# Start-up of a decayed cumulative sum of x @ w: another deal of channels to partitions, w by row sets, and other cuts of x

## The chip, the core and the metric

The kernel runs on one core of a Trainium2 chip. The metric is the device time of one execution in microseconds (us). Three executions of the kernel before took 902.97, 903.10 and 903.15 us, the median is 903.1. One more execution was profiled; all durations below come from it. A core has the matrix engine (PE, with its weight loads shown apart as PEld), the vector engine (DVE), the scalar engine (ACT), GpSimd (POOL) and a sync engine (SP) that here only issues transfers. ACT, POOL and SP each have a queue of DMAs.

## What is computed

```python
def reference(x, w, decay):          # x (16, 2048, 1024), w (1024, 1024), decay (1024), float32
    B, S, D = x.shape
    xw = x @ w
    out = np.zeros_like(xw)
    out[:, 0, :] = xw[:, 0, :].copy()
    for t in range(1, S):
        out[:, t, :] = decay[None, :] * out[:, t - 1, :] + xw[:, t, :]
    return out.astype(np.float32)
```

So there is one matrix product and then, for each output channel, a first-order recurrence over time.

## The kernel before

**Tiles.** Time is cut into chunks of 512 steps, 64 in all; two neighbouring chunks make a group. The product is made in bf16 with output channels on the partitions: a tile is 128 output channels by the 1024 steps of a group, eight tiles a group. One tile takes 16 matmuls of 512 columns: eight slices k of 128 input channels for each of the two chunks. For this x must stand with input channels on the partitions and time along the row.

**x.** `load` (L105) brings a chunk in four DMAs on POOL's queue, one for each quarter q of the input channels (256 of them) into 32 partitions; time runs over the 32 partitions and over j, 16 blocks of 32 steps. The DMA turns float32 into bf16. `turn` (L115) is DVE's transpose of 32 by 32 blocks, over pairs of bf16 taken as one 4-byte element; m counts four groups of 32 such pairs. Its result is `xw`, in which the even and the odd channel of a pair stand next to each other. `part` (L123) copies `xw` apart into `xt` (first all even, then all odd channels). A matmul (L131) reads either `xw` with a step of two (`pairs`) or `xt`. In the steady state one transpose handles a whole chunk (128 x 2048 elements), and there are 62 of those.

**w.** For a matmul the row of `wsb` on partition p must be the input channel that x has there. Before the change, partition 32q + i of slice (m, e) holds channel 256q + 64m + 2i + e. w comes in four pieces, by half h of the output channels and by e (even or odd input channels). `load_w` (L319) issues four DMAs a piece, one for each quarter q of 32 partitions, with the four m in it: 128 rows of 512 float32, 262 KB read. Piece (0, 0) goes as float32 over the queues of SP and ACT, two DMAs each; the other three pieces go over POOL's queue and arrive as bf16. `settle` (L326) copies a slice from its staging place to `wsb`; the even slices of the first half can only be settled when all four DMAs of their piece have landed.

**The recurrence.** A tile's sum is scanned on DVE, either directly from PSUM (L229) or in a paired form, in which ACT copies the tile from PSUM (L191, `p`), multiplies the even steps (L171, `g` and `h`), POOL adds (L205 and L266) and DVE scans half as many steps (L210). Then DVE transposes back (L278) and SP's queue stores.

**Order.** Every instruction is pinned to the order in which it is written. The first 49 steps and the last 20 follow an `agenda` written out by hand; entry -99 is the start. Its letters: M loads a part of x, U a piece of w on POOL's queue, w and W settle a slice on ACT or DVE (Q and q half a slice each), E transposes one m of a part, F and G copy one m to `xt` on DVE or ACT, K a small copy and matmul that wait for a quarter of x, L loads a quarter of a later chunk, R and D bring the decays. `cuts` says how the first two chunks are cut: chunk 0 into 10 and 6 blocks, chunk 1 into 7 and 9. Entry 3 holds the next work: among others `p0 g0` on ACT and then `w9 w10 w11`, three even slices of the second half of w, and `W8`, `W12` to `W15` on DVE.

**PE's start.** `spin` (L344) runs five matmuls with zeros in float32; the first one waits for ACT's copy into `seed` (L337), which stands behind ACT's two DMA issues and a table load. One more spin waits for `gate`, a copy that ACT makes when the last quarter of x's first part is there. Then step 0 runs the first half's four tiles on chunk 0 (`firsts`, in the parts of `cuts[0]`, all even slices of a part before the odd ones) and chunk 1 (`seconds`). In the second part of chunk 1 the first two tiles read `xw` and the other two `xt`. Step 4, the first with the second half of w, takes its even slices first.

**POOL's queue.** The built program gives the DMAs of this queue eight semaphores in turn: the ninth issue waits for the landing of the first, the tenth for that of the second, and so on.

Of the kernel before, what the change touches and what calls it, by code (L numbers as in the profile page):

```python
# [25 lines left out]
def kernel(  # L26
# [41 lines left out]
    CR = CH // NQ  # L68

# [40 lines left out]
    def turn(c, j0=0, j1=NJ, m0=0, m1=M):  # L110
        if c not in xw_of:
# [4 lines left out]
            out=dst.rearrange("p (m j i) -> p j m i", m=M, i=P)[:, j0:j1, m0:m1],  # L116
            in_=src.rearrange("p (j m c) -> p j m c", m=M, c=P)[:, :, m0:m1]))
# [168 lines left out]
    class Outlet:  # L286
# [8 lines left out]
        def store(self, b, t0):  # L295
# [4 lines left out]
            for j in range(0, self.nj, nj):  # L300
# [11 lines left out]
    stage = {(0, 0): room[0][:, 0:size],  # L312
             (0, 1): room[0][:, size:size * 3 // 2].bitcast(BF16),
             (1, 0): room[1][:, 0:size // 2].bitcast(BF16),
             (1, 1): room[1][:, size // 2:size].bitcast(BF16)}

    def load_w(queues, h, e):
        for i, q in enumerate((0, 2, 1, 3)):
            pin(queues[i % len(queues)].dma_start(  # L319
                out=stage[h, e][quad(q)].rearrange("p (m d) -> p m d", m=M),  # L320
                in_=_ap(w, [[2 * D, P], [2 * P * D, M], [1, CH]],
                        (q * CQ + e) * D + h * CH)))

    def settle(h, e, m, copy, r0=0, r1=R):
        src = stage[h, e][:, m * CH:(m + 1) * CH]
        pin(copy(out=wcols[:, 2 * m + e, h][:, :, r0:r1],  # L326
                 in_=src.rearrange("p (q r i) -> p q r i", q=NQ, r=R)[:, :, r0:r1]))
# [6 lines left out]
    load_w((nc.sync, nc.scalar), 0, 0)  # L334
# [11 lines left out]
    spin(5, seed, wide)  # L346
    H = NJ // 2
    cuts = (((0, H + 2), (H + 2, NJ)), ((0, H - 1), (H - 1, NJ)))
    cols = const.tile([128, 2, P], FP32, name="cols")

    def load_half(i):
        for q in range(NQ):
            load(i // 2, q, *cuts[i // 2][i % 2])
# [5 lines left out]
    def load_part(i):  # L359
        load_w((nc.gpsimd,), *((0, 1), (1, 0), (1, 1))[i])  # L360

    def part_one(i, copy):
        part(i // 8, copy, i % 4, i % 4 + 1, *cuts[i // 8][i // 4 % 2])
# [126 lines left out]
    def turn_and_load(c):  # L490
# [22 lines left out]
        "E": lambda i: turn(i // 8, *cuts[i // 8][i // 4 % 2], i % 4, i % 4 + 1),  # L513
# [132 lines left out]
    for step, (g, n) in enumerate(slots):  # L646
# [11 lines left out]
        if step == 0:  # L658
# [109 lines left out]
```

## Time and profile before

| what | us |
|---|---|
| median of three executions | 903.1 |
| the profiled execution's own time | 902.81 |
| its span, first to last recorded event | 901.0 |
| PE busy | 894.4 |
| DVE busy | 825.5 |
| ACT busy | 685.4 |
| POOL busy | 657.6 |

A group's row of the profile gives the line, the engine, the operation, its operands as out<-in with partitions x elements and type, how many there were, their busy time and the mean of one in ns, and the idle time before them with what ended it. A row of the timeline gives start, length, engine, line, operation and count of a run of instructions, and in brackets the idle time just before it. The sums that follow are made against the profiled execution; what is outside its span (1.81 us) is taken to stay.

Each DMA of the start, in float32 bytes read: a quarter of x takes 32.8 KB a block (10 blocks 328 KB, 6 blocks 197 KB), each w DMA 262 KB.

### The profile page before, as it was taken

To read this page: it belongs to the slowest core of one execution; us is meant where nothing else is said; L and a number is where in the kernel's file an instruction comes from. 1 tells how busy PE (TensorE), PEld (TensorE's weight loads), DVE (VectorE), ACT (ScalarE), POOL (GpSimd) and SP (SyncE) were. 2 spreads that over 40 slices of the span, in tenths; PEclk is the share of its full clock that TensorE was granted. 3 is DMA by queue.
4 is the path that set the end of the run, shared out by engine and by line. 5 is a ranking of instruction groups with operands and counts; after the bars stand their busy time and mean duration, and the time that the engine had idled before them with its cause. 6 is when DMAs were issued, how large, how long until landed. Compare 5 with 4: busy or idle time off the path is not lost.

```text
span 901.0 us, 12290 instructions
## 1 busy us (share of the span) xinstructions
PE 894.4 (99%) x4211; PEld 412.9 (46%) x4211; DVE 825.5 (92%) x635; ACT 685.4 (76%) x957; POOL 657.6 (73%) x758
## 2 busy tenths in 40 slices
PE   8999999999999999999999999999999999999998
PEld 5444444444444444444444444444444444444444
DVE  4899989999999999999998999989999999999998
ACT  4888878777877877877778778777787787787843
POOL 8887878877767768677677687777777777776532
PEclk9999999999999999999999999999999999999999
DMA  9999999999999999999999999999999999999648
GB/s 193 188 205 246 242 210 215 215 236 236 255 253 253 258 241 257 254 243 233 219 242 220 227 235 219 238 222 227 239 226 224 226 237 227 228 222 220 186 133 242
DMA packets 402798, 204.77 MB, mean 227 GB/s; under 512 B 9008, under 2 KB 401712, under 8 KB 402736
## 3 DMA queue, kind: packets, MB, share of 16 engines
q0 software_dynamic: 137024, 68.70, 57.5%
q1 hardware_dynamic: 265424, 134.76, 56.9%
q8 instruction: 33, 0.54, 0.2%
q10 hardware_dynamic: 288, 0.52, 0.2%
q14 instruction: 29, 0.24, 0.1%
HBM read 138.42 MB, written 134.22 MB: 303 GB/s over the span
## 4 chain that ended last, share of the span: by engine, by line
PE 99%; ACT 0%; ACTq 0%; DVE 0%; issue 0%
PE ps L131 97%; PE spare L131 1%; PE spare L344 1%; ACT L337 0%; PE ps L413 0%; PE spare L413 0%; ACTq L319 0%; DVE h L442 0%; ACT seed L337 0%
## 5 line engine op out<-in xcount | busy, mean ns | idle before, releaser
L131 PE MATMUL ps<-xt,wsb 128*128 128x512 bf16 (+2 forms) x4048 | 867.8, 377 | 0.0
L131 PEld LDWEIGHTS <-wsb 128*128 128x128 bf16 x4184 | 408.2, 98 | 477.0 <-issue 0.3
L205 POOL TENSOR_TENSOR xs<-h,xs 128x512 f32<-128x512 f32 (+1 forms) x190 | 242.6, 1278 | 181.8 <-ACT h L171 82.5
L278 DVE STREAM_TRANSPOSE ot<-so 128x1024 f32<-128x1024 f32 (+2 forms) x264 | 300.5, 1175 | 3.1 <-POOL so L266 2.2
L191 ACT COPY xs<-ps 128x1024 f32<-128x1024 f32 (+1 forms) x190 | 188.7, 994 | 149.6 <-PE ps L131 142.3
L266 POOL TENSOR_TENSOR so<-h,xs 128x512 f32<-128x512 f32 (+1 forms) x189 | 240.9, 1275 | 40.4 <-ACT h L171 27.4
L123 ACT COPY xt<-xw 128x2048 bf16<-128x2048 bf16 (+4 forms) x136 | 242.5, 1789 | 6.2 <-DVE xw L115 6.2
L105 POOL DMA_DIRECT2D xb<-in_x_dram x264 | 174.3, 661 | 8.4 <-DMA xb<-in_x_dram 3.5
L171 ACT ACTIVATE h<-so,dec 128x512 f32<-128x512 f32 (+1 forms) x189 | 144.8, 766 | 29.5 <-DVE so L210 26.2
L115 DVE STREAM_TRANSPOSE xw<-xb 128x2048 f32<-128x2048 f32 (+4 forms) x78 | 147.3, 1900 | 6.7 <-DMA xb<-in_x_dram 6.7
L210 DVE TENSOR_TENSOR_SCAN so<-spare,keep,xs 128x512 f32<-128x512 f32 (+1 forms) x97 | 119.8, 1239 | 26.5 <-POOL xs L205 25.9
L210 DVE TENSOR_TENSOR_SCAN so<-spare,xs 128x512 f32<-128x512 f32 x93 | 113.2, 1219 | 25.9 <-POOL xs L205 22.4
L171 ACT ACTIVATE h<-ps,dec 128x512 f32<-128x512 f32 (+1 forms) x190 | 129.5, 683 | 0.0
L229 DVE TENSOR_TENSOR_SCAN so<-dec,ps 128x1024 f32<-128x1024 f32 x34 | 76.9, 2261 | 0.8 <-ACT h L171 0.6
L229 DVE TENSOR_TENSOR_SCAN so<-dec,keep,ps 128x1024 f32<-128x1024 f32 (+2 forms) x35 | 74.9, 2140 | 0.8 <-PE ps L131 0.8
L270 ACT COPY keep<-so 128x1 f32<-128x1 f32 x136 | 25.3, 189 | 9.3 <-DVE so L229 8.7
L201 ACT COPY so<-keep 128x1 f32<-128x1 f32 x97 | 18.4, 191 | 4.3 <-DVE ot L278 4.1
L131 PE MATMUL spare<-xt,wsb 128*128 128x512 bf16 (+5 forms) x60 | 12.8, 330 | 0.0
L199 POOL MEMSET so<- 128x1 f32 x93 | 10.6, 115 | 2.7 <-DVE ot L278 2.7
L344 PE MATMUL spare<-wide,seed 128*128 128x512 f32 x10 | 7.5, 928 | 3.2 <-ACT seed L337 3.2
L131 PE MATMUL ps<-xw,wsb 128*128 128x288 bf16 (+4 forms) x64 | 10.5, 296 | 0.0
L319 POOL DMA_DIRECT2D ot<-in_w_dram x12 | 6.5, 547 | 0.8 <-issue 0.4
(44 smaller groups left out, 37.7 us busy)
## 6 DMA issues: line engine op xcount, KB each, us to landing
out_dram<-ot SPq DMA_DIRECT2D x236, 512.0 KB, 9.7
xb<-in_x_dram POOLq DMA_DIRECT2D x248, 256.0 KB, 7.6
out_dram<-ot SPq DMA_DIRECT2D x32, 256.0 KB, 4.4
ot<-in_w_dram POOLq DMA_DIRECT2D x12, 128.0 KB, 6.3
out_dram<-ot SPq DMA_DIRECT2D x8, 128.0 KB, 2.4
out_dram<-xb SPq DMA_DIRECT2D x3, 256.0 KB
xb<-in_x_dram POOLq DMA_DIRECT2D x4, 160.0 KB, 6.0
xb<-in_x_dram POOLq DMA_DIRECT2D x4, 144.0 KB, 4.6
```

Of the source, the lines that this page charges most:

```text
L105: pin(nc.gpsimd.dma_start(out=xb_of[c][quad(q), j0:j1], in_=_ap(x, [[D, P], [P * D, j1 - j0], [1, CQ]], (b * S + t0 + j0 * P) * D + q * CQ)))
L115: pin(nc.vector.transpose(out=dst.rearrange("p (m j i) -> p j m i", m=M, i=P)[:, j0:j1, m0:m1], in_=src.rearrange("p (j m c) -> p j m c", ...
L123: pin(copy(out=xt_of[c][:, m0:m1, :, j0 * P:j1 * P], in_=src))
L131: return pin(nc.tensor.matmul(out=ps[:, t0 % ps.shape[1]:][:, 0:t1 - t0], lhsT=lhs, rhs=rhs, start=(k == 0 and t0 == start), stop=(k == K ...
L171: pin(nc.scalar.activation(out=h[:, i * size:(i + 1) * size], in_=src, func=mybir.ActivationFunctionType.Copy, scale=dec[:, self.n:self.n ...
L191: pin(nc.scalar.copy(out=self.xs[:, i * size:(i + 1) * size], in_=ps))
L205: pin(nc.gpsimd.tensor_tensor(out=odds, in0=self.g, in1=odds, op=ALU.add))
L210: pin(nc.vector.tensor_tensor_scan(out=so[:, 3:T + 2:2], data0=squares[-1][:, n:n + 1].to_broadcast([128, T // 2]), data1=self.xs[:, 1:T:2 ...
L229: return pin(nc.vector.tensor_tensor_scan(out=so[:, t + 2:t + 2 + size], data0=dec[:, n:n + 1].to_broadcast([128, size]), data1=ps, initia ...
L266: pin(nc.gpsimd.tensor_tensor(out=self.so[:, 2:T + 2:2], in0=self.h, in1=self.xs[:, 0:T:2], op=ALU.add))
L270: pin(nc.scalar.copy(out=self.keep, in_=self.so[:, self.T + 1:self.T + 2]))
L278: pin(nc.vector.transpose(out=outlet.ot[:, :, c0:c0 + P], in_=self.so[:, 2 + t0:2 + t0 + nj * P].rearrange("p (i t) -> p i t", t=P)))
```

## The change

The channels are dealt out anew. With i = 8a + c, partition 32q + 8a + c of slice (m, e) now holds channel 256q + 64a + 16m + 2c + e. The 32 pairs of one m are therefore no longer next to each other in a row of `xb`, but come in four runs of eight, 32 elements apart, and `turn` reads them so, for all 64 chunks; its output is as before. On w's side all 128 partitions of one slice can now be written by one DMA: 16 groups of eight rows, so `load_w` loads slice by slice ("row sets"). Slices m = 0 and 1 of piece (0, 0) go as float32 over SP and ACT, one DMA each; m = 2 and 3 go over POOL's queue in bf16, as does piece (0, 1): six row sets ahead of the rest of x. The second half's eight row sets follow x. A `settle` then waits for its own slice's DMA.

Chunk 0 is cut into 12 and 4 blocks, chunk 1 into 5, 5 and 6; `seconds` gets a loop over the first two parts, so 32 matmuls with their weight loads are added. There are four zero spins in place of five. POOL's queue has 282 DMAs in place of 276. The order of entry -99 changes with it: the even slices 2 and 3 are settled on ACT before its first copies to `xt`; the copies of m = 0 and 1 of chunk 1 come later, behind others of ACT. The rest of the agenda is as it was.

```diff
+    IH = 4
+    IL = P // IH
...
         pin(nc.vector.transpose(
-            out=dst.rearrange("p (m j i) -> p j m i", m=M, i=P)[:, j0:j1, m0:m1],
-            in_=src.rearrange("p (j m c) -> p j m c", m=M, c=P)[:, :, m0:m1]))
+            out=dst.rearrange("p (m j a c) -> p m (j a) c", m=M, j=NJ, c=IL)[
+                :, m0:m1, j0 * IH:j1 * IH],
+            in_=src.rearrange("p (j a m c) -> p m (j a) c", a=IH, m=M, c=IL)[:, m0:m1]))
...
-    stage = {(0, 0): room[0][:, 0:size],
-             (0, 1): room[0][:, size:size * 3 // 2].bitcast(BF16),
+    early = room[0][:, 0:size // 2]
+    stage = {(0, 1): room[0][:, size:size * 3 // 2].bitcast(BF16),
              (1, 0): room[1][:, 0:size // 2].bitcast(BF16),
              (1, 1): room[1][:, size // 2:size].bitcast(BF16)}
-
-    def load_w(queues, h, e):
-        for i, q in enumerate((0, 2, 1, 3)):
-            pin(queues[i % len(queues)].dma_start(
-                out=stage[h, e][quad(q)].rearrange("p (m d) -> p m d", m=M),
-                in_=_ap(w, [[2 * D, P], [2 * P * D, M], [1, CH]],
-                        (q * CQ + e) * D + h * CH)))
+    stage[0, 0] = room[0][:, 0:size].bitcast(BF16)[:, size:2 * size]
+
+    def spot(h, e, m, count=1):
+        place = early if (h, e) == (0, 0) and m < 2 else stage[h, e]
+        return place[:, m * CH:(m + count) * CH]
+
+    def load_w(queue, h, e, m, count=1):
+        for i in range(m, m + count):
+            pin(queue.dma_start(
+                out=spot(h, e, i),
+                in_=_ap(w, [[2 * M * IL * D, NQ * IH], [2 * D, IL], [1, CH]],
+                        (2 * IL * i + e) * D + h * CH)))
 
     def settle(h, e, m, copy, r0=0, r1=R):
-        src = stage[h, e][:, m * CH:(m + 1) * CH]
+        src = spot(h, e, m)
...
-    load_w((nc.sync, nc.scalar), 0, 0)
+    load_w(nc.sync, 0, 0, 0)
+    load_w(nc.scalar, 0, 0, 1)
...
-    spin(5, seed, wide)
+    spin(4, seed, wide)
     H = NJ // 2
-    cuts = (((0, H + 2), (H + 2, NJ)), ((0, H - 1), (H - 1, NJ)))
+    cuts = (((0, 12), (12, NJ)), ((0, 5), (5, 10), (10, NJ)))
+    lots = [(c, *cut) for c in range(2) for cut in cuts[c]]
...
     def load_part(i):
-        load_w((nc.gpsimd,), *((0, 1), (1, 0), (1, 1))[i])
+        h, e, m, count = i // 8, i // 4 % 2, i % 4, 2 if i < 8 else 4
+        load_w(nc.gpsimd, h, e, m, count)
+
+    def turn_one(i):
+        c, j0, j1 = lots[i // 4]
+        turn(c, j0, j1, i % 4, i % 4 + 1)
...
-        -99: "M0 U0 M1 M2 M3 U1 U2 w0 W1 w2 W3 K3 E0 E1 G0 E2 G1 E3 F2 G3 Q4 q4 W5 W6 W7 E4 E5 G4 E6 G5 E7 F6 G7 R E8 E9 G8 E10 G9 E11 F10 G11 E12 L E13 G12 L E14 G13 E15 L F14 G15 D",
+        -99: "M0 U2 U4 U6 M1 M2 M3 M4 U8 U12 w0 W1 K3 E0 E1 E2 w2 w3 E3 G0 F2 G1 W4 W5 F3 W6 W7 E4 G4 E5 E6 G5 E7 F6 G7 R E8 E9 E10 G10 E11 F11 G8 E12 E13 E14 G14 E15 F15 G9 L E16 G16 E17 G12 L F17 E18 G18 E19 G13 L F19 D",
...
-            Q = cuts[1][0][1] * P
-            for k0 in range(0, K, 2):
-                for i in range(R):
-                    for k in (k0, k0 + 1):
-                        matmul(seconds[i], i, k, xt_of[1], 0, Q,
-                               pairs=xw_of[1] if k0 < 4 else None)
+            for j0, j1 in cuts[1][:2]:
+                for k0 in range(0, K, 2):
+                    for i in range(R):
+                        for k in (k0, k0 + 1):
+                            matmul(seconds[i], i, k, xt_of[1], j0 * P, j1 * P, j0 * P,
+                                   pairs=xw_of[1] if k0 < 4 else None)
+            Q = cuts[1][2][0] * P
```

More of the change, by code (lines that the diff above doesn't have):

```diff
@@ L352, in load_half @@
         for q in range(NQ):
-            load(i // 2, q, *cuts[i // 2][i % 2])
+            load(lots[i][0], q, *lots[i][1:])
     def spin_on(q):
@@ L512 @@
         "r": await_settled,
-        "E": lambda i: turn(i // 8, *cuts[i // 8][i // 4 % 2], i % 4, i % 4 + 1),
+        "E": turn_one,
         "F": lambda i: part_one(i, nc.vector.tensor_copy),
```

3 lines of the change are left out of this document (2 added, 1 removed).

## The prediction

> **What bounds the kernel now.** I read the page's busy shares first, then the chain that ended last, then the timeline of each engine up to 27 us, then the windows up to 100 us.
>
> ```profile
> PE 894.4 (99%) x4211; PEld 412.9 (46%) x4211; DVE 825.5 (92%) x635; ACT 685.4 (76%) x957; POOL 657.6 (73%) x758
> ...
> 3.22 7.76 PE spare L344 x11
> ...
> 42.50 830.65 PE ps L131 x3848
> ```
>
> The chain is PE from 3.22 us to the end. From 42.50 us it runs 3848 matmuls in 830.65 us, 215.9 ns each, without a gap that the profile shows. So the time is the moment of PE's first real matmul, plus a fixed stream, plus whatever PE waits after that. The change can only move the first and the last.
>
> ```profile
> 0.75 0.91 ACTq L319 DMA_DIRECT2D ot<-in_w_dram  x2
> 1.69 1.28 ACT L337 ACT_TABLE_LOAD   x1 [1.69 <-PEq L752]
> 2.98 0.19 ACT L337 COPY seed<-wide 128x1 f32<-128x1 f32 x1
> 9.72 0.19 ACT L356 COPY gate<-xb 32x1 bf16<-32x1 bf16 x1 [1.78 <-DMA xb<-in_x_dram]
> ...
> 20.49 1.82 ACT L123 COPY xt<-xw 128x576 bf16<-128x576 bf16 x3 [1.65 <-DVE xw L115]
> 22.29 1.01 ACT L191 COPY xs<-ps 128x1024 f32<-128x1024 f32 x1
> 23.20 0.69 ACT L171 ACTIVATE h<-ps,dec 128x512 f32<-128x512 f32 x1
> 23.94 1.66 ACT L326 COPY wsb<-ot 128x512 bf16<-128x512 bf16 x3
> ```
>
> ACT's two DMA issues hold the table load, and that holds the first spin at 3.22 us. `gate` was ready at 9.91 us. At 22.29 us the copy `p0` starts right after ACT's last copy to `xt`, then `g0`, then w9 to w11 end at 25.60 us.
>
> ```profile
> 10.61 0.38 PE L344 MATMUL spare<-wide,gate 128*128 128x512 bf16 x1
> 10.82 0.59 PE L131 MATMUL ps<-xw,wsb 128*128 128x320 bf16 x3
> ...
> 21.07 2.20 PE L131 MATMUL ps<-xw,wsb 128*128 128x288 bf16 x16
> ...
> 25.07 2.11 PE L131 MATMUL ps<-xt,wsb 128*128 128x512 bf16 x9
> ```
>
> Real work starts at 10.82 us. The first transpose (below) was done near 9.76 + 0.48 = 10.24 us, so the spins held PE for about half a microsecond. The second half of w starts at 25.07 us.
>
> ```profile
> 9.76 1.69 DVE L115 STREAM_TRANSPOSE xw<-xb 128x320 f32<-128x320 f32 x4 [2.16 <-DMA xb<-in_x_dram]
> ...
> 12.45 0.86 DVE L326 COPY wsb<-ot 128x256 bf16<-128x256 bf16 x4 [0.62 <-DMA ot<-in_w_dram]
> 14.50 1.16 DVE L115 STREAM_TRANSPOSE xw<-xb 128x192 f32<-128x192 f32 x4 [1.19 <-DMA xb<-in_x_dram]
> ...
> 16.89 1.29 DVE L115 STREAM_TRANSPOSE xw<-xb 128x224 f32<-128x224 f32 x4 [0.92 <-DMA xb<-in_x_dram]
> ...
> 19.98 1.56 DVE L115 STREAM_TRANSPOSE xw<-xb 128x288 f32<-128x288 f32 x4 [1.47 <-DMA xb<-in_x_dram]
> ```
>
> All of these wait for DMAs. The steps between them are transfer times: piece (0, 1) of w, 1.05 MB, in 2.69 us; 0.79, 0.92 and 1.18 MB of x in 2.05, 2.39 and 3.09 us. That is 0.38 to 0.39 MB/us throughout, so the start is a stream of DMA, and PE's lead over it is thin: x's last part gives its first transposed m at 19.98 + 0.45 = 20.43 us, and PE wants it at 21.07.
>
> ```profile
> 10.64 4.95 POOL L105 DMA_DIRECT2D xb<-in_x_dram  x8 [0.16 <-issue]
> 15.58 2.71 POOL L319 DMA_DIRECT2D ot<-in_w_dram  x5
> ...
> 50.00:60.00 10.00, 10.00 (x48) 4.53 (x47) 10.00 (x8) 8.03 (x14) 9.88 (x12) 1.00 1.16 178
> ```
>
> POOL pays 0.62 us for each x DMA and 0.54 for each w DMA. In the last row (length, then PE, PEld, DVE, ACT, POOL) DVE has no idle time, so a lead of PE that DVE doesn't follow may be given back there.
>
> **The start of PE.** One issue on ACT in place of two takes 0.45 us off the first spin; a single issue of the new shape could cost up to both old ones, so 0 to 0.45. One zero spin is two weight loads fewer: their starts stand 0.43 us apart late (9.32, 9.75) and 0.86 early, so 0.86 to 1.7, of which I take 0.86, since the last ones go. Spins thus end 1.3 us earlier, near 9.3. Then x decides. Up to its first part the stream now holds 0.52 + 1.57 = 2.10 MB against 1.05 + 1.31 = 2.36, so by 0.385 MB/us it lands 0.7 us before 9.64 (the wait at 9.72 less its 0.08), at 8.95. If POOL's queue does not begin sooner, although SP and ACT carry half as much, it is 0.26 MB later: 10.3. I take 9.2, nearer the first, as both queues share one stream. The first transpose of 384 takes 0.54 (0.346 and 0.481 for 192 and 320 give 1.05 ns an element), so PE starts at 9.9 in place of 10.82: **0.9 us won**, between 1.2 (spins) and -0.1.
>
> **Work added on PE.** 32 matmuls with their loads cost nothing but their fixed part. Four 192-column matmuls take 0.35 us and 512 columns 0.216, so the fixed part is 2 to 7 ns: 0.1 us in all. Parts of 384, 128, 160, 160 and 192 columns then take 5.3, 1.8, 2.25, 2.25 and 2.7 us, 14.3 together, as the 14.25 before.
>
> **The transposes in runs of eight.** No row here reads runs of eight. The small ones read runs of 32, the 62 large ones one run, and both cost 1.04 ns an element ((2283 - 481) ns over 1728), so no gain is left below. Upper bound: a scan's 2261 ns for 1024, two cycles an element. I take nothing, by the nearest row. The scan that reads every second element costs 1219 ns for 512, as the contiguous ones (1209): a step is not charged either.
>
> **w by row sets.** Each set moves the same 262 KB as a quarter did, and the quarters already moved at the stream's rate, so spreading has little left to give: 0.66 us a set. Bounds: 0.60 and 0.87 (the slowest 0.30 MB/us, of the mixed first phase). The Trainium skill, DMA: Bandwidth & Descriptors, section Latency and other measured facts, speaks against: at row pitches of large powers of two copies slow down, 207 GB/s at 512 KiB and 164 at 2 MiB against 214. Here 16 groups lie 256 KiB apart; by that table (my estimate) a set would cost 3% more at most, 0.68 us, and the sum would come out 0.2 us longer. No run here shows that pitch.
>
> **POOL's queue, the step that costs.** With x's first part at 9.2 and six sets at 0.66, the last set lands at 13.2. x's chunk 1 goes in twelve smaller DMAs. Through the eight semaphores its fourth issue waits for that set: 13.2 + 0.6 = 13.8. The other eight follow at 0.57 each (POOL's rows for 6 to 10 blocks, 0.56 to 0.62): 18.4. The last lands after that by between 0.5 (its own transfer of 197 KB) and 3.15 us (the shortest w DMA of POOL took 3.7 from issue, less 0.54). I take 2.3, nearer the measured end: 20.7 in place of 19.98. The stream forbids less than 19.6. The second half of w is issued behind these and lands in time slice by slice: its first set near 21.3, wanted past 24.
>
> PE now reaches that part at 9.9 + 11.6 = 21.5. m = 0 is there at 21.05, but DVE puts a copy between the second and third m, so m = 2 is done at 21.9 and m = 3 at 22.2; PE waits 0.2 us and reaches the second half of w at 24.4. On ACT, queued behind this late part are four copies to `xt` (0.42 us steps), until 22.8; behind them `p0`, `g0` and w9 to w11, by the rows above 2.25, 2.8 and 3.3 us from p0's start: 25.05, 25.6 and 26.1. PE wants them 0.43, 0.86 and 1.3 us after its start there, 24.8, 25.25 and 25.7. It waits in steps, in sum about 0.45, and with the 0.2 before and a 0.1 for semaphores **0.75 us is given back**, between 0 (landing at 19.6) and 1.6 (21.5). DVE is not late: `W8` waits for one set and not for four DMAs, so its scan at 24.17 comes a little sooner. After 30 us the later loads queue behind the same bytes.
>
> **Sum.** -0.9 + 0.75 = -0.15 us: 902.66 against the profiled 902.81. The median of the runs stood 0.29 above that execution, so 902.95. What a measurement of this kernel tells from no change I set at 0.2%, 1.8 us; the forecast is no change. Its own range is -1.2 to +1.5.
>
> **Rivals.**
> *The start is won whole.* If the last part lands at 19.6, ACT's chain fits and -0.9 stays: 902.2. For it: the same bytes landed by 19.98 before. Against: POOL's issue time for twelve small DMAs.
> *The row sets come slower.* At 0.87 us a set the six are 1.3 us late, x behind them too, and PE's waits grow by 1.3: 904.3. The Trainium skill's rule on pitches (DMA: Bandwidth & Descriptors, the section named above) would make it 903.15 by itself. For this rival: 16 engines step through rows with one distance; against: the old quarters had 256 KiB between their m as well and reached 0.39 MB/us.
> *The runs of eight cost a second cycle (slower).* Place: L115, in every chunk. 62 x 2.13 us makes DVE's 825.5 into 957.6; with the some 14 us up to 24 us that it must idle, the time is about 972. It decides from about 0.3 us a transpose, since in the windows from 60 to 100 us DVE was busy 39.1 of 40. Against: the two prices above, equal for runs of 32 and for one run.
> That spreading w over the engines does nothing is no rival of its own: the sum has it.
>
> **Chances.** No change as summed 0.66; start won whole 0.14; slower sets 0.14, half of it beyond 904.9; costly runs 0.06. A gain over 1.8 us needs PE to start by 9.0, before the spins end: 0.03. Slower by over 1.8: 0.06 + 0.07 + 0.02 from the forecast's own far end = 0.15. Within: 0.82. The range 901.8 to 905.0 leaves out the costly runs, the worst of the sets and the far gain.
>
> **What would show it.** Right: first real matmul near 9.9; first spin near 2.8; large transposes still at 2283 ns; x's last transpose group at 20.7; gaps on PE only between 21 and 27 us, some 0.7 us in sum; then 215.9 ns a matmul. Wrong: a transpose group over 2.5 us, `gate` after 10.3, or a gap after 30 us, where I let DVE follow for nothing.

## The result and the profile after

The changed kernel takes 906.38 us in the median of seven executions (905.59 to 906.63); the kernel before, timed beside it, 903.15 (902.97 to 903.85). The ratio is 1.0032, with a 95% interval of 1.0021 to 1.0044: 0.3% slower, beyond the noise, where no change was forecast (902.95, at most 905.0). The profiled execution took 906.55 us with a span of 904.8, against 902.81 and 901.0.

The timeline of ACT and of PE in the changed kernel (start, length, engine, line, operation and count; in brackets the idle time just before):

```profile
0.75 0.66 ACTq L327 DMA_DIRECT2D ot<-in_w_dram  x1
...
10.73 0.19 ACT L366 COPY gate<-xb 32x1 bf16<-32x1 bf16 x1 [5.23 <-DMA xb<-in_x_dram]
...
26.31 1.00 ACT L194 COPY xs<-ps 128x1024 f32<-128x1024 f32 x1
...
27.80 1.65 ACT L334 COPY wsb<-ot 128x512 bf16<-128x512 bf16 x3
```

```profile
2.97 6.25 PE L353 MATMUL spare<-wide,seed 128*128 128x512 f32 x8 [2.97 <-ACT seed L346]
10.98 0.39 PE L353 MATMUL spare<-wide,gate 128*128 128x512 bf16 x1 [1.75 <-ACT gate L366]
11.40 1.02 PE L134 MATMUL ps<-xw,wsb 128*128 128x384 bf16 x3
...
28.00 15.06 PE L134 MATMUL ps<-xt,wsb 128*128 128x512 bf16 x66
...
63.38 11.81 PE L134 MATMUL ps<-xt,wsb 128*128 128x512 bf16 x53 [0.35 <-DVE so L232]
```

The spins start 0.25 us sooner than before and end at 9.22, but `gate` comes at 10.73 in place of 9.72, PE idles 1.75 us, and real work starts at 11.40 in place of 10.82. The second half of w starts at 28.00 in place of 25.07: 2.93 us lost up to there. (The second half of w is here always PE's step with that name, short "w2" in the tables below; the agenda's `w2` is another thing.) Behind it the waits for w9 to w11 cost 0.40 us (the starts of matmuls stand 0.47, 0.29 and 0.29 apart in place of 0.216), and one gap at 63 us, where PE waits for a scan of DVE, 0.51 (from start to start 0.725 in place of 0.216). That makes 3.84, the 3.8 of the spans.

The timelines of DVE and of POOL:

```profile
10.77 1.96 DVE L117 STREAM_TRANSPOSE xw<-xb 128x384 f32<-128x384 f32 x4 [6.25 <-DMA xb<-in_x_dram]
...
16.15 0.89 DVE L117 STREAM_TRANSPOSE xw<-xb 128x128 f32<-128x128 f32 x4 [1.22 <-DMA xb<-in_x_dram]
...
17.81 1.02 DVE L117 STREAM_TRANSPOSE xw<-xb 128x160 f32<-128x160 f32 x4 [0.47 <-DMA xb<-in_x_dram]
...
21.34 1.02 DVE L117 STREAM_TRANSPOSE xw<-xb 128x160 f32<-128x160 f32 x4 [2.14 <-DMA xb<-in_x_dram]
...
24.18 0.64 DVE L117 STREAM_TRANSPOSE xw<-xb 128x192 f32<-128x192 f32 x2 [1.46 <-DMA xb<-in_x_dram]
```

```profile
8.97 0.51 POOL L327 DMA_DIRECT2D ot<-in_w_dram  x1 [1.54 <-DMA xb<-in_x_dram]
9.96 0.57 POOL L107 DMA_DIRECT2D xb<-in_x_dram  x1 [0.47 <-DMA xb<-in_x_dram]
10.93 1.19 POOL L107 DMA_DIRECT2D xb<-in_x_dram  x2 [0.40 <-DMA xb<-in_x_dram]
12.29 7.65 POOL L107 DMA_DIRECT2D xb<-in_x_dram  x13 [0.17 <-issue]
```

x's last part is transposed from 24.18 us, where the kernel before began at 19.98. POOL issues thirteen DMAs of x in a row, 0.59 us each, until 19.94. The chain of waits in the changed kernel, followed back from the gap at 63 us (start, length, what), no longer runs through PE at the start:

```profile
1.31 1.96 POOL xb L107 x3
3.27 7.38 DMA xb<-in_x_dram
...
10.93 0.56 POOL xb L107
...
14.89 4.47 POOL xb L107 x8
19.37 4.73 DMA xb<-in_x_dram
24.18 0.65 DVE xw L117 x2
...
27.02 2.19 DVE so L232
...
61.01 2.33 DVE so L232
63.38 2.75 PE ps L134 x12
```

It is x's first part (until 10.65), POOL's issues, x's last part (until 24.10), then DVE, whose scans are late from 27 us on and hold PE at 63. Lastly the windows (length; busy PE, PEld, DVE, ACT and POOL; granted clock, DMA share, GB/s written), of the kernel before and then of the changed one:

```profile
12.00:15.00 3.00, 3.00 (x24) 2.10 (x23) 1.36 (x6) 0.78 (x3) 2.95 (x6) 1.00 1.45 192
15.00:18.00 3.00, 3.00 (x37) 2.92 (x35) 2.08 (x9) 1.91 (x5) 3.00 (x6) 1.00 1.44 192
18.00:21.00 3.00, 3.00 (x34) 2.94 (x32) 1.53 (x5) 1.35 (x3) 2.15 (x5) 1.00 1.32 195
```

```profile
12.00:15.00 3.00, 3.00 (x11) 1.39 (x10) 2.58 (x8) 2.09 (x3) 2.59 (x6) 0.51 1.28 185
15.00:18.00 3.00, 3.00 (x20) 1.76 (x19) 1.38 (x7) 1.02 (x3) 3.00 (x6) 1.00 1.16 144
18.00:21.00 3.00, 3.00 (x48) 2.87 (x47) 1.16 (x5) 0.82 (x2) 3.00 (x7) 1.00 1.14 132
```

x and w arrive at half their size, so 192 GB/s written are the 0.385 MB/us of float32 of the prediction. Before, that rate holds throughout. After, it falls to 144 from 15 to 18 us and to 132 from 18 to 21, three quarters and two thirds; from 19 to 20 us alone it is 96. And PE runs at a granted clock of 0.51 from 12 to 15 us, behind its pause.

### The profile page after: what moved, and what is told of

The parts are those of the page before. It is cut to its first block, busy times and chain, and to the rows that moved or that the text cites. A ratio compares the mean times of both kernels' runs of the same rounds, so it can differ in the third digit from the quotient of the medians.

```text
span 904.8 us, 12268 instructions
## 1 busy us (share of the span) xinstructions
PE 891.5 (99%) x4160; PEld 412.8 (46%) x4241; DVE 827.5 (91%) x641; ACT 685.8 (76%) x958; POOL 660.8 (73%) x764
## 4 chain that ended last, share of the span: by engine, by line
PE 92%; DMA 2%; DVE 2%; POOL 2%; issue 1%; ACT 0%; DVEq 0%; POOLq 0%
PE ps L134 91%; DMA xb<-in_x_dram 2%; POOL xb L107 1%; DVE so L232 1%; PE spare L134 1%; DVE ot L281 1%; POOL xs L208 0%; DVE so L213 0%; ACT h L174 0%; ACT xs L194 0%; DVE xw L117 0%; DVE wsb L334 0%; PE ps L429 0%; PE spare L429 0%; POOL so L269 0%
## 5 line engine op out<-in xcount | busy, mean ns | idle before, releaser
L107 POOL DMA_DIRECT2D xb<-in_x_dram x268 | 176.2, 659 | 5.1 <-DVE xw L117 2.2
L117 DVE STREAM_TRANSPOSE xw<-xb 128x2048 f32<-128x2048 f32 (+4 forms) x82 | 147.7, 1815 | 12.3 <-DMA xb<-in_x_dram 11.5
L134 PE MATMUL ps<-xw,wsb 128*128 128x160 bf16 (+4 forms) x76 | 12.3, 294 | 0.4 <-DVE xw L117 0.4
```

The source lines that it names most:

```text
L107: pin(nc.gpsimd.dma_start(out=xb_of[c][quad(q), j0:j1], in_=_ap(x, [[D, P], [P * D, j1 - j0], [1, CQ]], (b * S + t0 + j0 * P) * D + q * CQ)))
L117: pin(nc.vector.transpose(out=dst.rearrange("p (m j a c) -> p m (j a) c", m=M, j=NJ, c=IL)[:, m0:m1, j0 * IH:j1 * IH], in_=src.rearrange(" ...
L134: return pin(nc.tensor.matmul(out=ps[:, t0 % ps.shape[1]:][:, 0:t1 - t0], lhsT=lhs, rhs=rhs, start=(k == 0 and t0 == start), stop=(k == K ...
```

## The experiments

Eighteen kernels, each timed beside the kernel before on the same chip; the median of that one was 902.7 to 903.5 in these groups. Single executions of the kernel before ran from 902.3 to 904.5 us. "x last" is the start of the first transpose of x's last part and "w2" the start of PE's second half of w, both from the profiled execution.

| kernel | median us | ratio to before, 95% | x last | w2 |
|---|---|---|---|---|
| before | 903.15 | 1 | 19.98 | 25.07 |
| changed | 906.38 | 1.0032 (1.0021 to 1.0044) | 24.18 | 28.00 |
| e1 six spins | 906.88 | 1.0048 (1.0036 to 1.0061) | 24.20 | 28.02 |
| e2 two parts of chunk 1 | 906.35 | 1.0043 (1.0030 to 1.0055) | 23.54 | 29.89 |
| e3 four row sets on SP, ACT | 907.55 | 1.0049 (1.0036 to 1.0061) | 24.66 | 28.46 |
| e4 deal alone | 904.84 | 1.0020 (1.0011 to 1.0029) | 22.86 | 27.70 |
| e5 transposes alone | 903.37 | 1.0002 (0.9993 to 1.0011) | 22.16 | 27.00 |
| e6 e4, quarters on SP, ACT | 902.90 | 0.9998 (0.9989 to 1.0007) | 20.63 | 25.47 |
| e7 e4, quarters on POOL | 904.24 | 1.0014 (1.0005 to 1.0023) | 21.96 | 26.80 |
| e8 before, four spins | 903.01 | 1.0001 (0.9992 to 1.0010) | 19.82 | 24.66 |
| e9 changed, halves on SP, ACT | 906.91 | 1.0040 (1.0026 to 1.0053) | 24.75 | 28.56 |
| e10 changed, quarters on SP, ACT | 905.61 | 1.0023 (1.0014 to 1.0032) | 23.41 | 27.22 |
| e11 before, cut 12/4 | 904.77 | 1.0015 (1.0007 to 1.0024) | 23.00 | 27.83 |
| e12 e6, three parts of chunk 1 | 904.75 | 1.0011 (1.0002 to 1.0020) | 23.39 | 27.20 |
| e13 changed, decays first | 906.52 | 1.0041 (1.0029 to 1.0054) | 24.10 | 28.02 |
| e14 e2, decays first | 906.01 | 1.0035 (1.0023 to 1.0048) | 23.49 | 28.32 |
| e15 before, decays first | 903.00 | 1.0001 (0.9992 to 1.0010) | 20.16 | 24.99 |
| e16 e11, chunk 1 in one part | 908.64 | 1.0062 (1.0046 to 1.0079) | 21.87 | - |
| e17 changed, chunk 1 in one part | 910.89 | 1.0086 (1.0071 to 1.0101) | 23.11 | - |
| e18 e13, DVE's copies on ACT | 906.29 | 1.0038 (1.0024 to 1.0052) | 23.93 | 27.74 |

Two things hold through the table. Where chunk 1 has two parts, the profiled execution's time is w2 plus 877.7 to 877.8 us in all ten kernels; with three parts 0.2 to 0.8 more. And w2 is x's last part plus 4.83 or 4.84 in all of the two-part kernels but two, and plus 3.80 to 3.92 with three parts. The two are the kernel before (5.09: there PE came to x's last part 0.25 us after x) and e2 (below). So the landing of x's last part sets the time in nearly all of them. (e16 and e17 have chunk 1 in one part and another order of work, so these sums don't apply.)

**The pause of PE (e1).**

```diff
-    spin(4, seed, wide)
+    spin(6, seed, wide)
```

> The changed kernel with six zero spins in place of four, so that PE is busy until x's first part is there. In the changed kernel PE paused 1.75 us before the gate and then ran its first 384-column matmuls at 0.32 us until about 14.8, later ones at 0.16; the first part took 6.9 us. Clock theory (the pause costs speed): the spins end near 10.9, the real start stays near 11.4, the matmuls run at 0.16 from the start and the first part ends near 16.7 in place of 18.31. If the last parts of x had slack, all 1.6 us would reach the end: 904.9. Lateness theory (x's last part, transposed at 24.18, is a wall of its own): PE then waits before the second and third part of chunk 1, the second half of w starts near 27.3 in place of 28.00, and the time is 905.8 against 906.5. If the slow matmuls come from something else (the DMAs, the even steps of xw): 906.5 and still 0.32 us.

```profile
11.26 0.39 PE L353 MATMUL spare<-wide,gate 128*128 128x512 bf16 x1 [1.33 <-ACT gate L366]
11.69 0.67 PE L134 MATMUL ps<-xw,wsb 128*128 128x384 bf16 x3
...
16.99 0.33 PE L134 MATMUL ps<-xw,wsb 128*128 128x128 bf16 x3
```

In this timeline of e1's PE the first part takes 16.99 - 11.69 = 5.30 us, 1.6 less than in the changed kernel's profile, though a pause of 1.33 us was left. w2 stays at 28.02: the 1.6 us vanish in waits for x's later parts. The time didn't fall at all, less than even the lateness theory had it. So the low clock was real, but it was hidden: x's lateness cost the time. The changed kernel's own executions say the same: three of the seven have a mean granted clock of 0.998 like the profiled one (3 us at half speed are about 0.002 of 905 us) and took 905.59 to 906.55 us; four have 0.999 or 1.000 and took 905.91 to 906.63. Seven more kernels paused longer than 1.75 us before a first part at full speed (last section).

**Which part of the change makes x late (e3, e4, e5, e6, e7).** First the deal by itself, and its row sets for SP and ACT in the changed kernel.

```diff
-    load_w(nc.sync, 0, 0, 0)
-    load_w(nc.scalar, 0, 0, 1)
+    for i in range(M):
+        load_w((nc.sync, nc.scalar)[i % 2], 0, 0, i)
```

> The changed kernel with all four even row sets of the first half of w on SP's and ACT's queues, two each, as float32; POOL's queue carries two DMAs fewer ahead of x's rest. Stream theory, as the prediction had it: 0.52 MB more go ahead of x's first part, which lands 1.4 us later, near 12.1, PE starts near 12.7, and the end moves by +0.5 to +1.4 us: 907.0 to 908.0. Queue theory (POOL's queue delivers less than the stream until about 8 us whatever the others do, so what SP and ACT carry meanwhile is free): x's first part lands within 0.5 us of 10.7, the odd sets 1.3 us sooner, the last part of x some 1.1 us sooner, the first spin starts 0.6 us later (one more issue on ACT) and ends near 9.9, so the pause shrinks to about 1 us: 904.5 to 905.5.

x's first part was transposed from 12.13 us and the time was 907.55, as the stream theory said; e10 below shows that this was not for its reason.

e4 has these lines too, with `spin(5)`, the cuts of before and its order (`U0` is then `U4 U6`, `U1 U2` is `U8 U12`).

> The kernel before with the new deal alone: transposes in runs of eight in all 64 chunks and w by row sets, four for each piece, but the cuts, the spins, the order and the division between the queues of before. By the prediction's terms (runs of eight 0, a row set 0.66 us as a quarter): as before, 903.1, within 0.5. If spreading w over the engines is worth something: down to 902.5. Rival, the row sets come slower or cost the engines more: PE starts late and the time is 904 or more. If the deal itself carried the loss, 906.

The deal alone costs 0.20%, 1.8 us: the rival. The next three take it apart.

```diff
# e5, in the kernel before
-            out=dst.rearrange("p (m j i) -> p j m i", m=M, i=P)[:, j0:j1, m0:m1],
-            in_=src.rearrange("p (j m c) -> p j m c", m=M, c=P)[:, :, m0:m1]))
+            out=dst.rearrange("p (m j a c) -> p m (j a) c", m=M, j=NJ, c=IL)[
+                :, m0:m1, j0 * IH:j1 * IH],
+            in_=src.rearrange("p (j a m c) -> p m (j a) c", a=IH, m=M, c=IL)[:, m0:m1]))
# e6, in e4 (load_quarters is load_w of before); e7 has it in load_part
-    for i in range(M):
-        load_w((nc.sync, nc.scalar)[i % 2], 0, 0, i)
+    load_quarters((nc.sync, nc.scalar), 0, 0)
```

> The kernel before with one edit: the transposes of all 64 chunks read x in runs of eight. w stays as it was, so the product pairs other channels of x with the rows of w; the amount of work is the same. The deal alone took 904.8 against 902.7 in the run before this one. If its loss is in the row sets of w: no change here, 902.7 within 0.7, the large transposes at 2283 ns and the parts of x transposed from 9.8, 14.5, 16.9 and 20.0 us as in the kernel before. If the transposes carry it: 904.8.

> The deal alone (second run of its kind: old cuts, order and spins), but the first even piece of w goes over SP's and ACT's queues in quarters of 32 partitions again, while POOL's queue keeps its row sets. The rows of that piece so come to other partitions than x's channels; the work is the same. Theory H (the four row sets on SP and ACT start later, at 0.65 to 0.79 us an issue against 0.43, and set the sixteen engines apart before x begins): the landings of each x DMA are again within 0.6 us, x's parts are transposed from 9.8, 14.5, 16.9 and 20.0 us, time 902.7 to 903.3. Theory P (it is POOL's row sets that set the engines apart): shares of one DMA land 1.6 us apart as with the deal alone, x's last part near 22.9, time 904.5 to 905.

> The deal alone with its four row sets on SP and ACT, but POOL's queue loads the three other pieces of w in quarters again (rows on other partitions than x's channels, same work). Theory H: the first spin at 3.6 us as with the deal alone, engines apart by 1.6 us, x's parts transposed from 11.2, 15.8, 18.2 and 22.9 us, time 904.5 to 905. Theory P: 902.7 to 903.3 and engines within 0.6 us once SP's and ACT's DMAs are through. Something between would mean that both add.

The transposes are free: 1.0002, and in the profile's groups of e5 the large ones still take 2284 ns:

```profile
L117 DVE STREAM_TRANSPOSE xw<-xb 128x2048 f32<-128x2048 f32 x62 | 141.6, 2284 | 0.5 <-DMA xb<-in_x_dram 0.5
```

POOL's row sets are free too (e6: 0.9998). The row sets on SP and ACT are not (e7, with four of them: 1.0014, 1.2 us by the medians, just short of what its theory H forecast). SP's timeline of e4, then of e6:

```profile
0.75 1.57 SPq L325 DMA_DIRECT2D ot<-in_w_dram  x2
```

```profile
0.75 0.86 SPq L332 DMA_DIRECT2D ot<-in_w_dram  x2
```

An issue of a row set takes SP 0.79 us against 0.43 for a quarter, and the four DMAs had landed by 8.98 us in e4 against 6.64 in e6. x comes behind them: its first part landed at 11.07 and 10.00. (e5's profile is of one execution that took 904.7 us, the longest of its eleven; x's last part came at 22.16 in it, with nothing changed but the free transposes. The start varies by itself.)

**SP's and ACT's share in the changed kernel (e9, e10).**

```diff
# e9, in the changed kernel
-    load_w(nc.sync, 0, 0, 0)
-    load_w(nc.scalar, 0, 0, 1)
+    for i, queue in enumerate((nc.sync, nc.scalar)):
+        pin(queue.dma_start(
+            out=early[i * 64:(i + 1) * 64].rearrange("p (m d) -> p m d", m=2),
+            in_=_ap(w, [[2 * D, 64], [2 * 64 * D, 2], [1, CH]], 4 * 64 * i * D)))
# e10, in e6
-    cuts = (((0, 10), (10, NJ)), ((0, 7), (7, NJ)))
+    cuts = (((0, 12), (12, NJ)), ((0, 5), (5, 10), (10, NJ)))
-    spin(5, seed, wide)
+    spin(4, seed, wide)
```

> The changed kernel with one edit: its two DMAs on SP and ACT bring 64 partitions by two slices each in place of 128 partitions by one (other rows of w on these partitions, so other products; same bytes, same places, same waits). With the deal alone, row sets on SP and ACT cost 0.65 to 0.79 us an issue against 0.43 and the kernel 1.3 to 1.8 us; with quarters there (sixth run) that was gone. If the shape of these DMAs is what sets the engines apart in the changed kernel too: issue 0.43, first spin near 2.7, the landings of the second quarter of x within 0.8 us (1.9 in the changed kernel), first transpose near 9.7, time 904.0 to 905.0. If POOL's queue starts unevenly when it is alone, whatever went before: first transpose still near 10.7, landings 1.5 us apart and more, time 906.0 to 906.6.

> The changed kernel (deal, cuts 12/4 and 5/5/6, its order, four spins) with all four DMAs of the first even piece on SP and ACT and in quarters of 32 partitions, as the kernel before has them (other rows of w on these partitions; POOL's queue carries two w DMAs fewer ahead of x's rest). The fourth-but-one kind, with four row sets there, took 907.6. If these row sets are the loss: x's first part lands with the stream, 0.26 MB at 0.385 MB/us after 9.64, near 10.3, real work near 11.0, last part of x near 21, time 903.2 to 904.0. If the cuts carry a loss of their own: 905.0 or more, with x's first part at 10.3 all the same and a wait for x's last parts.

e9 decides little: ACT's issue took 0.71 us in this shape too, and nothing got better. e10 carries all four DMAs on SP and ACT in quarters and loses 2.2 us to the kernel before, where the changed kernel loses 3.2; that is the second of its forecasts, in which the cuts carry a loss of their own. Its first part of x, 12 blocks, landed at 10.83, after 1.05 MB of w; in the changed kernel it landed at 10.65 after 0.52 MB. The 0.52 MB taken from SP and ACT bought 0.2 us. e3 differs from e10 only in the shape of these four DMAs. So e3's 12.01 was not the bytes, as the stream theory has it, but their coming in row sets.

**The cuts and the spin (e2, e8, e11, e12).**

```diff
# e2, in the changed kernel (the order of chunk 1 as before)
-    cuts = (((0, 12), (12, NJ)), ((0, 5), (5, 10), (10, NJ)))
+    cuts = (((0, 12), (12, NJ)), ((0, 7), (7, NJ)))
# e8, in the kernel before
-    spin(5, seed, wide)
+    spin(4, seed, wide)
# e11, in the kernel before
-    cuts = (((0, H + 2), (H + 2, NJ)), ((0, H - 1), (H - 1, NJ)))
+    cuts = (((0, 12), (12, NJ)), ((0, H - 1), (H - 1, NJ)))
# e12, in e6 (the order of chunk 1 as in the changed kernel)
-    cuts = (((0, 10), (10, NJ)), ((0, 7), (7, NJ)))
+    cuts = (((0, 10), (10, NJ)), ((0, 5), (5, 10), (10, NJ)))
```

> The changed kernel with chunk 1 in two parts of 7 and 9 blocks, eight DMAs in place of twelve, and four spins as it has. Issue theory (POOL's 0.59 us for each small DMA keeps x's last part late): four issues fewer, the last x DMA is issued near 17.6 in place of 19.94, its first transpose stands near 21 in place of 24.18, PE meets no wait there, reaches the second half of w near 27.3 in place of 28.00, and the waits for w9 to w11 (0.4 us in sum) and for DVE at 63 us (0.5) get smaller: 905.0, between 904.6 and 905.8. Stream theory (the same bytes at the rate the engines allow): the last part stays near 24 and the time at 906.5. The pause and the slow first part stay in both.

> The kernel before with four zero spins in place of five and nothing else. In the kernel before the first transpose was done near 10.24 us and the spins held PE until 10.82. By the prediction's term for the start: the spins end 0.86 us earlier, PE's real start moves to about 10.35, the stream of x has room for it (first transposed m of the last part at 20.43 against 20.6 wanted), the second half of w starts near 24.6 in place of 25.07, and the time falls by 0.3 to 0.45 us: 902.3 against 902.7. Rival: the pause before the gate makes PE start at half speed, as in the profile of the changed kernel (0.32 us for a 384-column matmul until 3.4 us after the start): the first part takes 1.5 us longer and the time is 903.5 to 904.

> The kernel before with chunk 0 cut into 12 and 4 blocks and nothing else. The first part is 0.26 MB larger: it lands 0.7 us later, near 10.3, its first transpose is done 0.07 us later still, PE starts 0.6 to 0.7 us later (the spins had 0.1 to 0.6 us to spare), and as PE's stream is fixed the time grows by 0.5 to 0.7: 903.5 to 903.7 against 903.0. If later waits swallow it (the second half of w or x's last part bind anyway): 903.0. If it unsettles POOL's queue as in the changed kernel: 904.5 or more.

> The sixth run's kernel (deal, quarters on SP and ACT, cuts of before; 902.9 against 903.0 there) with chunk 1 in parts of 5, 5 and 6 blocks, four x DMAs more, and the order that goes with them; same rows of w as there. Issue theory: four more issues at 0.57 us put x's last part at 21.5 to 22.5 in place of 20.6, PE waits up to 1 us there and ACT's copies w9 to w11 come late: 903.5 to 904.3. If the eight small DMAs keep pace (stream theory): 902.7 to 903.2. In the changed kernel two parts in place of three changed nothing (906.35 against 906.4), which speaks for the second.

Each cut costs 1.4 us by the medians when it is made alone (the stream theory gave 0.6 for the one, nothing for the other), and undoing the second in the changed kernel (e2) gains nothing. e11 is the case in which the cut unsettles POOL's queue; e12 lies beyond both of its forecasts. Read as a ladder, the medians' losses to the kernel before are -0.1 us for the deal with quarters on SP and ACT (e6), 1.4 with three parts of chunk 1 as well (e12), 2.2 with the cut 12/4 and four spins as well (e10), and 3.2 for the changed kernel, which besides brings the first even piece of w in row sets, half of them over POOL's queue. Each of these figures is good to about 1 us by its interval, so the steps of 0.9 and 1.0 are not sure one by one, and in another order they would have other prices, as e2 shows. e8 wins 0.4 us in its profile (w2 at 24.66), as forecast for this term, but the median doesn't show it. e11's chain of waits has no PE ahead of x's last part either:

```profile
3.27 7.75 DMA xb<-in_x_dram
...
13.91 2.44 POOL xb L105 x4
16.36 6.52 DMA xb<-in_x_dram
...
23.00 0.49 DVE xw L115
```

The next table sets the kernels side by side by when the DMAs of x had landed (the trace records sixteen shares of each; last share, us; one profiled execution each):

| | first part | chunk 0 | chunk 1 | chunk 1's 2.10 MB took |
|---|---|---|---|---|
| e8 | 9.60 | 14.26 | 19.69 | 5.4 |
| before | 9.64 | 14.38 | 19.85 | 5.5 |
| e15 | 9.84 | 14.49 | 20.03 | 5.5 |
| e6 | 10.00 | 14.55 | 20.51 | 6.0 |
| e5 | 10.24 | 14.90 | 22.04 | 7.1 |
| e12 (three parts) | 10.08 | 14.74 | 23.27 | 8.5 |
| e10 (three parts) | 10.83 | 14.81 | 23.28 | 8.5 |
| e11 | 11.02 | 15.02 | 22.87 | 7.8 |
| e7 | 10.80 | 15.46 | 21.83 | 6.4 |
| e4 | 11.07 | 15.69 | 22.74 | 7.0 |
| changed (three parts) | 10.65 | 16.02 | 24.10 | 8.1 |

The kernel before seems to stand at an edge. With chunk 0 landed 0.1 to 0.2 us later, chunk 1 still comes at about the full rate (2.10 / 0.385 = 5.5 us). With 0.5 us and more, or in three parts, it takes 1 to 3 us longer. The delay of chunk 0 is not the whole rule: e7's came 0.4 us after e11's, and its chunk 1 took 1.4 us less. And e5, whose median is that of the kernel before, shows that a single execution can fall over the edge by itself. So the costs of the parts need not add up: 1.2 (e7, with four row sets on SP and ACT, where the changed kernel has two), 1.4 (e11) and 1.4 (e12) alone, 3.2 together. Up to the end of chunk 0 the kernel before and the changed one load the same 4.2 MB (1.05 on SP and ACT, 1.05 of w on POOL's queue and 2.10 of x; then 0.52, 1.57 and 2.10), and the changed one needs 1.6 us more for it; chunk 1 adds 2.6.

**What holds chunk 1 (e13 to e18).** Three suspects were tried. The first, four small DMAs of decay on SP's queue near 17 us:

```diff
# e13; e14 and e15 the same in e2 and in the kernel before
-        -99: "M0 U2 ... G7 R E8 ...
+        -99: "R M0 U2 ... G7 E8 ...
```

> The changed kernel with the four DMAs of decay at the start of SP's queue (right behind its one w DMA, near 1.5 to 2.8 us) in place of near 17.4 us. Theory of the decays (SP's DMAs hold up POOL's descriptors some 2 us later): the rate no longer falls to 170 to 220 GB/s near 19 to 20 us, x's last part lands 1 to 1.5 us sooner (first transpose of it near 23 in place of 24.18), and the time falls to 905.2 to 905.9 from 906.4. Theory of the dry queue (small DMAs, 0.57 us an issue and 1.7 us until the first share lands): the dip stays, 906.4 within 0.4. A cost of its own at the start, where SP's queue now has more: first transpose later than 10.77, time above 906.5.

> The second run's kernel (the changed kernel with chunk 1 in parts of 7 and 9 blocks, 906.35) with the DMAs of decay at the start. There x's last part was transposed at 23.54, its four DMAs landing in steps of 1.15, 1.37, 1.61 and 0.82 us though 0.76 us is what 9 blocks take of the stream. Theory of the decays: steps of 0.8 us, last part near 21.7, second half of w near 26.3 in place of 27.8, time 904.3 to 905.0. Theory of the dry queue: unchanged, 906 to 906.6.

> Control: the kernel before with the DMAs of decay at the start. Its DMA rate shows no dip after 12 us, so neither theory expects a change from the place near 16 us: 903.0 within 0.4. If four small DMAs ahead on SP's queue cost the start something: first transpose later than 9.76 and up to 0.5 us more.

No effect in any: x's last part stood at 24.10, 23.49 and 20.16 us, 0.2 us at most from where it was, and the times are those forecast for no effect. The second, the number of POOL's DMAs:

```diff
# e16, in e11; e17 the same in the changed kernel
-    cuts = (((0, 12), (12, NJ)), ((0, H - 1), (H - 1, NJ)))
+    cuts = (((0, 12), (12, NJ)), ((0, NJ),))
```

> The kernel before with chunk 0 cut into 12 and 4 and chunk 1 in one part of 16 blocks: four DMAs of 0.52 MB in place of eight. With the cut 12/4 alone (the eleventh run) x's last byte of chunk 1 landed at 22.88, after 15.03 for chunk 0. Theory of the dry queue: four issues of 0.65 us keep POOL ahead of the stream, the rate stays near 0.385 MB/us, and 2.10 MB after 15.0 land by 20.5 (20.2 to 21.0), no rate under 300 GB/s between 15 and 20 us; PE then has chunk 1's 7.2 us left, so the second half of w starts near 28.5 and the time is 906.0 to 906.6. If something else slows the engines near 19 us: landed at 22 or later, time 907.8 or more.

> The changed kernel with chunk 1 in one part of 16 blocks: four DMAs in place of twelve. In the changed kernel chunk 0 had landed at 16.02 and chunk 1 at 24.10. Theory of the dry queue: chunk 1 lands by 21.5 (21.2 to 22.2); the second half of w starts near 29.5 and the time is 907.0 to 907.8. If something else slows the engines: landed at 23.5 or later, time 909 or more.

Chunk 1 had landed at 21.75 and 23.03, between the two forecasts, later than the first. The times, 908.64 and 910.89, are those of the second forecast, but they hold a loss of clock too: PE waited 4.12 and 4.80 us for x, and its clock was then 0.50 for some 3 us. The windows of e16:

```profile
12.00:15.00 3.00, 3.00 (x20) 1.73 (x19) 2.45 (x9) 1.85 (x4) 2.96 (x6) 1.00 1.38 186
15.00:16.50 1.50, 1.50 (x11) 0.91 (x10) 0.82 (x5) 1.02 (x3) 1.50 (x4) 1.00 0.54 55
16.50:21.00 4.50, 2.02 (x34) 1.84 (x32) 0.00 (x0) 0.00 (x0) 1.31 (x3) 1.00 1.39 188
```

For 1.5 us the rate falls to 55 GB/s and the DMA share from 1.38 to 0.54, though POOL had issued the three DMAs that come next by 14.17 us. So the pace of the issues is not the whole cause, and POOL was not short of issued DMAs: the first of the three, issued by 12.76 us, had no share landed before 17.61. The third suspect, DVE's copies:

```diff
# e18, in e13
-... G0 F2 G1 W4 W5 F3 W6 W7 ... F6 ... F11 ... F15 ...
+... G0 G2 G1 w4 w5 G3 w6 w7 ... G6 ... G11 ... G15 ...
```

> The changed kernel with the DMAs of decay at the start (the thirteenth run, 906.52) and with DVE's copies between 12 and 20 us moved to ACT: two copies to xt of the first part, four slices of w, and one copy to xt for each of the parts (0, 1), (1, 0) and (1, 1) that DVE made. DVE keeps the transposes. ACT gets 0.8 + 0.8 + 4 x 0.6 + 0.4 x 3 = 5.2 us more where it idled 6 us, so PE waits for odd slices of w in its first part. Theory of the copies (POOL's DMAs issued while DVE copies come into work late): no rate under 250 GB/s between 15 and 22 us, x's last part follows its last issue (near 19.8) by the 1.7 us of an empty queue and its own share, last byte by 22.5 in place of 24.02 to 24.10, its first transpose near 22.6 in place of 24.10; the time then hangs on ACT and PE: 905.0 to 906.5. If the copies are innocent: the falls stay, last byte at 23.8 or later, time 906.5 or more. In a sentence of its own: the Trainium skill, SBUF - State Buffer, section SBUF: two separate sides, states that while DVE runs a copy in its two-port mode GpSimd cannot write the descriptors of the DMAs that it issues; no run so far shows that by itself.

```profile
15.00:18.00 3.00, 2.39 (x14) 1.29 (x15) 1.18 (x6) 3.00 (x7) 3.00 (x6) 1.00 1.11 137
18.00:21.00 3.00, 3.00 (x48) 2.81 (x47) 0.73 (x4) 1.85 (x6) 3.00 (x7) 1.00 1.15 127
```

In these windows of e18 DVE makes no copy, and the rate is as low as in the changed kernel (144 and 132); chunk 1's last byte came at 23.85, the innocent side of what was expected (the time, 906.29, is 0.2 us under that side's bound). The Trainium skill (SBUF — State Buffer, section SBUF: two separate sides) describes such a stall, in which a DVE copy keeps GpSimd from writing the descriptors of its DMAs; these falls come without one.

What stays open is what the DMA engines wait for in these falls. One candidate was seen and not tried: DVE's transposes of a part just landed run at the start of several of the falls. Against it: the kernel before runs such transposes from 14.50 and 16.89 us, and its rate stays at 192 GB/s.

## Why the prediction was wrong

Forecast were 0.9 us won at the start and 0.75 given back; measured were 2.93 us lost up to the second half of w, then 0.40 for w9 to w11 and 0.51 for DVE. Two terms failed: the time of x's first part, and, dearer, that of x's last part, which sets when PE reaches the second half of w. The steps in its order:

- **The first spin** was put near 2.8 and came at 2.97: ACT's one issue took 0.66 us, not half of the old two. The spins ended at 9.22 (9.3).
- **x's first part at 9.2 us failed**, and the bound of 10.3 with it: 10.65. The step counted SP's, ACT's and POOL's bytes as one stream of 0.385 MB/us, so that 0.26 MB less would come 0.7 us sooner. POOL's queue did start sooner, its first share landed at 5.57 in place of 6.47, but alone, behind SP's and ACT's DMAs (landed by 4.86), it took 2.06, 0.99 and 0.97 us for the next three quarters of 0.39 MB. Why the second took twice as long as the others stays open. e10 agrees: 0.52 MB more on SP and ACT, 0.2 us later. The 0.9 us won became 0.58 lost.
- **Parts of 14.3 us** were right at full clock (e1: 5.30 and 1.80 for the first two, against 5.3 and 1.8). That a pause could lower the clock was not in the sum; here it cost 1.6 us that x's lateness hid.
- **Transposes at nothing**: right (2284 ns; e5). **A row set at 0.66 us**: right on POOL's queue (0.61 to 0.71 from landing to landing in the changed kernel; e6). The rival of slower sets was wrong about the rate. What row sets cost is on SP and ACT, by the issue and by when they land; of this only ACT's issue was among the terms.
- **POOL's queue**: the pace was right (the last eight issues took 4.48 us, 0.56 each), but they started 1.7 us late, with x's first part and the sets behind it. **x's last part 2.3 us after its last issue failed**: 4.16 us, beyond the bound of 3.15, and 24.10 in place of 20.7. So of the 3.4 us that x's last part came late, 1.5 are the start of these issues and 1.9 the landing. The bound itself was misread: the 3.7 us are those of a w DMA on SP's queue (3.68); POOL's shortest w DMA before took 4.90 from issue, and its DMAs of x there landed 3.54 us and more after their issue's end, the last of chunk 1 4.26. Nor is the delay a price of one DMA, as the step took it. In the changed kernel the five DMAs issued from 14.20 to 16.57 us had landed 2.2 to 2.5 us after their issue, as forecast; the five behind them took 3.35 to 4.16, when the rate fell to 96 GB/s. What went with it is how far POOL is ahead: from the end of an issue to its first landed share the kernel before never has less than 2.9 us up to chunk 1's end; the changed kernel has 1.6 to 2.0 from 12.3 us on, about the least that any run shows (1.6). That the short lead makes the rate fall is not shown: in e16 it fell and stayed low with three DMAs issued long enough before. What makes it fall stays open.
- **ACT's chain** behind x's last part was right in its steps: p0 to the end of w11 took 3.14 us (3.3), and the waits there 0.40 (0.45). They came 3.5 us later.
- **DVE follows for nothing** failed: 0.51 us at 63 us, the sign named for it. Its late scans stand in the chain.
- The **0.6 us of lead** that PE seemed to have on x's last part was the key reading. Of the 0.64 us, a real slack of 0.25 was left in the rows (5.09 against 4.84), and the whole kernel was within that of being bound by x's DMA.

## What to carry to other kernels

When an engine at 99% is fed by a queue with little lead, the queue is the second bound, and a change to the start should be costed by what it does to that lead. Bytes over a rate didn't forecast it here, nor did a fixed delay from issue to landing; read that delay from rows of the same queue, and look how far the issues are ahead of the landings at each DMA. Bytes taken off one queue are not time won: here 0.52 MB less on SP and ACT bought 0.2 us. And parts that each cost a little alone, near such an edge, cost no sum: try them one by one and together.

## What the runs showed of the hardware that was not expected

**The length of a pause doesn't settle the clock after it.** PE paused before its real work 1.75 us in the changed kernel, and its clock fell to 0.51 for about 3 us; pauses of 1.33 (e1), 1.82 (e10), 1.89 (e2, e11), 2.33 (e9), 2.74 (e13), 2.81 (e17) and 3.15 us (e3) in the same place left the first part at full speed. After 3.19 us (e14) the clock fell only 1.5 us into the first part, to 0.50 from 13 to 16 us. Of the seven executions of the changed kernel four seem to have kept the full clock (e1, above). In e2 a second pause, of 1.78 us at 22 us, lowered it again, as its windows show:

```profile
24.00:27.00 3.00, 2.93 (x14) 1.79 (x14) 2.13 (x9) 2.94 (x5) 2.77 (x5) 0.65 1.23 199
```

That is why its w2 stands 6.35 us after x's last part. The Trainium skill (TensorE: Matmul & The Clock Gate, Part 1) has a window of about 3.4 us that runs freely, one idle window of which lowers the clock. That the window runs freely fits the scatter; that a whole one must be idle does not: pauses of half its length were enough twice.

**The shares of one DMA drift apart.** The sixteen shares of a quarter of x landed within 0.5 to 0.9 us in the kernel before, and 1.7 to 1.9 us apart in the changed kernel for its second and third quarter; the next DMA that POOL may issue waits for the last of them.

**The same bytes cost SP and ACT different issues**: 0.43 to 0.46 us for 32 partitions by four rows, 0.65 to 0.79 for 128 partitions by one, 0.71 to 0.73 for 64 by two (e9).
